# Moving the on-chip tiles of a two-block layer so that activation slots and weight buffers start at one place modulo 512 bytes

## The chip, the core and the metric

The kernel runs on one core of a Trainium2 chip. The metric is the device time of one execution in microseconds. A core has TensorE for matrix products (the profile splits it into PE, the matmuls, and PEld, the weight loads that run ahead of them), VectorE (DVE), ScalarE (ACT), GpSimd (POOL) and SyncE (SP), which only issues transfers here. Operands lie in the on-chip memory SBUF, whose 128 partitions all use the same byte address for one element of a tile; products are summed in PSUM.

## The reference

Two transformer-like blocks follow each other on 256 tokens of width 2048, all in float32. Nearly all the work is products of a 256-row activation with large weights:

```python
def first_block(x, p, w_in, ...):
    h = rmsnorm(x, g_mix[i])
    proj = h @ w_in[i]                       # 2048 x 10240
    y_sb = stick_breaking_attention(q_sb, k_sb, v_sb)
    y_ca = chunked_relpos_attention(q_ca, k_ca, v_ca, rel_bias[i])
    merged = (sigmoid(gate_sb) * (y_sb @ w_sb_out[i]) + sigmoid(gate_ca) * (y_ca @ w_ca_out[i]))
    x = x + merged @ w_mix_out[i]
    g_ff, u_ff = split(rmsnorm(x, g_ffn[i]) @ w_ffn_in[i], 2)      # 2048 x 11264
    x = x + (silu(g_ff) * u_ff) @ w_ffn_out[i]
    x = x + sigmoid(rmsnorm(x, g_ple[i]) @ w_ple_gate[i]) * (p[i] @ w_ple_in[i])
    return rmsnorm(x, g_final)

def second_block(x, ...):
    proj = rmsnorm_2(h, norm_mix_w[l]) @ w_in[l]                   # 2048 x 13328
    y_a, y_b, y_c = s5_branch(...), gla_branch(...), diff_attn_branch(...)
    merged = g0 * y_a + g1 * y_b + g2 * y_c
    h = h + merged @ w_out[l]
    h = h + conv_gated_mlp(rmsnorm_2(h, norm_ffn_w[l]), ffn_w_up[l], ..., ffn_w_down[l])
    return rmsnorm_2(h, norm_final_w)
```

## The kernel before

**The stream of weights.** All weights pass through one loop, `stream` (L448 to L537), in tiles of 128 x 1024 floats. SyncE loads a tile into one of four `raw` buffers (L459); ScalarE rounds it to a high part `wh`, one of five buffers (L466); VectorE takes the difference `wl`, one of four buffers (L476). TensorE then multiplies with the high and the low part, so that a product keeps more digits than one pass gives. These passes read `float32r` operands, at one column per step of the clock.

**The activations.** An activation is split in the same way and kept in slots of 8192 bytes in each partition, fifteen of them (`NSLOT = 15`, L187). A slot of class `Acts` holds four k-tiles, each as 256 columns of high part and 256 of low part. The same fifteen slots hold every other intermediate too. `try_slot` (L208) hands out the first free one, so which slot a product reads is fixed when the program is built.

**Two kinds of products.** A matmul reads two operands from SBUF: the stationary one, 128 columns, which a weight load puts into the array ahead of the matmul, and the moving one, up to 512 columns.

- Kind AS, `mm_as` (L555 to L562): the slot is stationary, the weight buffer is moving, 512 columns each; three matmuls for each k-tile and half (L560, L561, L562).
- Kind WS (L522 to L532): the weight buffer is stationary, the slot is moving; for each k-tile and half one matmul of 256 columns with `wl` (L530) and one of 512 columns with `wh` (L526).

While matmul number i streams its moving operand, the weight load of number i+1 reads its stationary operand: one of the two reads is always from a slot, the other from a `wh` or `wl` buffer.

**Where tiles lie.** Tiles get addresses pool by pool, in the order in which the pools are opened (L192 to L194): `one`, `raw`, `wh`, `wl`, `ev`. Within a pool tiles follow each other in the order of their first use, each rounded up to 32 bytes. The fifteen slots are tiles of the pool `one` (L212), which also holds small tiles (`r`, `rh`, `ss`, `nv`, `lam`: 8 to 48 bytes), the residual `big` (16384 bytes), the parameters `par` (L580, 832 bytes), constants `cst` (1536 bytes) and `tri`/`rel`/`conv` (L589, 1376 bytes). The slots therefore start at different places modulo 512, wherever a small tile came between.

Of the kernel before, what the change touches and what calls it, by code (L numbers as in the profile page):

```python
# [9 lines left out]
F32 = mybir.dt.float32  # L10
# [149 lines left out]
class Flag:  # L160


    def __init__(self, tile=None):
        self.tile, self.ready = tile, False
# [21 lines left out]
class Build:  # L186
    NSLOT = 15  # L187

    def __init__(self, tc, d, out, es):
        self.tc, self.nc, self.d, self.out = tc, tc.nc, d, out  # L190
        pool = lambda name, bufs, **kw: es.enter_context(tc.tile_pool(name=name, bufs=bufs, **kw))
        self.one = pool("one", 1)  # L192
        self.rawp, self.whp, self.wlp = pool("raw", RAWB), pool("wh", CA + 1), pool("wl", SA + 1)
        self.ev = pool("ev", 2)  # L194
        self.accp = pool("acc", 2, space=PSUM)
        self.psp = pool("ps", 1, space=PSUM)
        self.drp = pool("dr", 1, space=bass.MemoryType.DRAM)
        self.psfree, self.cooling, self.ticks = [0, 1, 2, 3], [], 0
        self.slotfree = list(range(self.NSLOT))
        self.gens, self.lanes, self.nm = [], {}, 0  # L200
        self.tab, self.forced, self.nrb = None, 0, 0
# [6 lines left out]
    def try_slot(self, shape, dtype=F32):  # L208
        if not self.slotfree:
            return None  # L210
        i = self.slotfree.pop(0)
        return self.one.tile(shape, dtype, tag=f"s{i}", name=self.name("s")), i  # L212

    def slot(self, shape, dtype=F32):
        while True:
# [209 lines left out]
        rb.ready = True  # L425

    def new_norm(self, with_rb=True):
        r = Flag(self.one.tile([128, 2], F32, tag=self.name("r"), name=self.name("r")))
        r.half = self.one.tile([128, 2], F32, tag=self.name("rh"), name=self.name("rh"))
        rb = None  # L430
        if with_rb:
            self.nrb += 1
            rb = Flag(self.one.tile([128, 256], F32, tag=f"rb{self.nrb % 2}", name=self.name("rb")))
        ss = self.one.tile([128, 2, 4], F32, tag=self.name("ss"), name=self.name("ss"))
        return r, rb, ss
# [141 lines left out]

    def consts(self):
        nc, d, one = self.nc, self.d, self.one
        self.par = one.tile([128, P_N], F32, tag="par", name="par")  # L580
        self.cst = one.tile([128, C_N], F32, tag="cst", name="cst")
        nc.sync.dma_start(out=self.par, in_=d["par"])
        c = self.cst
        self.ident, self.ones, self.BT = (c[:, o:o + 128] for o in (C_ID, C_ONE, C_BT))
        self.one1 = c[:, C_ONE:C_ONE + 1]
# [1182 lines left out]
```

## Time and profile before

| | |
|---|---|
| median of 3 runs | 3183.13 us (3182.76 to 3183.58) |
| the profiled execution, its own time | 3182.36 us |
| its span, first to last instruction | 3180.2 us |
| PE busy | 3161.4 us, 99% of the span |
| PEld busy | 2668.2 us, 84% |
| DVE busy | 1994.4 us, 63% |
| ACT busy | 1553.3 us, 49% |
| DMA engines, queue that SyncE issues on | 55.8% |
| matmuls of kind AS (L560, L561, L562) | 3 x 2372 |
| matmuls of kind WS (L526, L530) | 2 x 3936 |

Busy time is time in which at least one instruction of the engine is under way. The recorded duration of one matmul holds its way through the array as well, so that records overlap: what a matmul costs in a stream is the distance from its start to the next one's start, and a group's first and last start, divided by the number of steps between them, gives that distance.

### The profile page before, as it was taken

The numbers are of one execution on the slowest core, as the hardware profiler recorded it, in microseconds if no ns is written. First come the engines' busy times: TensorE is split into PE (matmuls) and PEld (weight loads), VectorE is DVE, ScalarE is ACT, GpSimd is POOL, SyncE is SP. The second block draws the span as 40 slices with busy tenths as digits, with TensorE's granted clock in tenths as the row PEclk, the third lists the DMA queues.
The fourth block names the chain that finished last, engine by engine and source line by source line (L and its number), as shares of the span: only waits on it lengthen the run. The fifth ranks groups of instructions, "written<-read, shape, count | busy, mean of one in ns | idle before, by whom it ended". The sixth has DMA issues, their size and how long they took to land.

```text
span 3180.2 us, 43735 instructions
## 1 busy us (share of the span) xinstructions
PE 3161.4 (99%) x16909; PEld 2668.2 (84%) x16909; DVE 1994.4 (63%) x2593; ACT 1553.3 (49%) x2035; POOL 72.5 (2%) x158
## 2 busy tenths in 40 slices
PE   8999999999999999999999999999999999999998
PEld 7888888888888888888888888878888888888887
DVE  5656445557577676566655657945555766757666
ACT  6544444455444454456544454434445644545545
POOL 0000000000001000000000001000000000000000
PEclk9999999999999999999999999999999999999999
DMA  7555555565667767555654565655555555555554
GB/s 263 168 176 166 185 188 183 180 187 186 216 223 246 243 225 238 186 175 190 210 178 159 170 214 192 211 183 198 197 183 182 186 192 185 186 195 185 189 185 165
DMA packets 172639, 617.90 MB, mean 194 GB/s; under 512 B 23552, under 2 KB 23968, under 8 KB 169232
## 3 DMA queue, kind: packets, MB, share of 16 engines
q1 hardware_dynamic: 164992, 577.49, 55.8%
q0 software_dynamic: 7440, 37.64, 3.5%
q8 instruction: 132, 2.16, 0.3%
q14 instruction: 75, 0.61, 0.1%
HBM read 599.74 MB, written 14.25 MB: 193 GB/s over the span
## 4 chain that ended last, share of the span: by engine, by line
PE 99%; ACT 0%; DMA 0%; DVE 0%; DVEq 0%; issue 0%; SPq 0%; ACTq 0%
PE acc L526 29%; PE acc L560 17%; PE acc L562 17%; PE acc L561 17%; PE acc L530 15%; PE p L346 1%; PE p L1673 0%; PE p L1132 0%; PE p L1713 0%; PE p L906 0%; PE p L908 0%; PE p L907 0%; PE p L1716 0%; PE p L1109 0%; PE p L1128 0%; PE p L1707 0%
## 5 line engine op out<-in xcount | busy, mean ns | idle before, releaser
L476 DVE TENSOR_TENSOR wl<-raw,wh 128x1024 fp32r<-128x1024 f32 x1088 | 1320.6, 1220 | 667.1 <-PE acc L561 446.0
L466 ACT CAST wh<-raw 128x1024 fp32r<-128x1024 f32 x1088 | 1138.9, 1049 | 1110.3 <-PE acc L562 672.1
L526 PE MATMUL acc<-s,wh 128*128 128x512 f32 x3936 | 1383.8, 396 | 0.0
L530 PE MATMUL acc<-s,wl 128*128 128x256 f32 x3936 | 1090.6, 282 | 0.0
L560 PE MATMUL acc<-wh,s 128*128 128x512 f32 x2372 | 939.0, 396 | 0.8 <-DVE big L1351 0.8
L562 PE MATMUL acc<-wh,s 128*128 128x512 f32 x2372 | 930.8, 392 | 0.0
L561 PE MATMUL acc<-wl,s 128*128 128x512 f32 x2372 | 930.3, 392 | 0.0
L526 PEld LDWEIGHTS acc<-s,wh 128*128 128x128 f32 x3936 | 734.1, 188 | 164.0
L530 PEld LDWEIGHTS acc<-s,wl 128*128 128x128 f32 x3936 | 741.7, 188 | 11.0 <-issue 1.0
L562 PEld LDWEIGHTS acc<-wh,s 128*128 128x128 f32 x2372 | 445.6, 188 | 99.9
L560 PEld LDWEIGHTS acc<-wh,s 128*128 128x128 f32 x2372 | 445.9, 188 | 99.2 <-issue 1.7
L561 PEld LDWEIGHTS acc<-wl,s 128*128 128x128 f32 x2372 | 446.0, 188 | 97.5 <-issue 0.5
L442 DVE TENSOR_TENSOR s<-acc,s 128x512 f32<-128x512 f32 (+1 forms) x120 | 82.7, 689 | 271.1 <-ACT s L441 271.0
L441 ACT COPY s<-acc 128x512 f32<-128x512 f32 (+1 forms) x120 | 70.0, 584 | 195.0 <-PE acc L526 192.8
L310 ACT ACTIVATE s<-s 128x256 f32<-128x256 f32 (+4 forms) x175 | 76.6, 443 | 105.2 <-DVE s L313 38.1
L313 DVE SCALAR_TENSOR_TENSOR s<-s,conv 128x256 f32<-128x256 f32 x172 | 79.4, 482 | 3.1
L444 DVE TENSOR_TENSOR s<-s,rb 128x512 f32<-128x512 f32 (+1 forms) x104 | 71.7, 690 | 3.5
L318 ACT CAST s<-s 128x256 fp32r<-128x256 f32 (+1 forms) x104 | 45.5, 442 | 30.4 <-DVE s L946 15.3
L1630 DVE TENSOR_TENSOR s<-s,s 128x1024 f32<-128x1024 f32 x48 | 58.5, 1219 | 0.0
L310 ACT ACTIVATE s<-s,conv 128x256 f32<-128x256 f32 x86 | 47.1, 595 | 22.5 <-DVE s L444 22.5
L319 DVE TENSOR_TENSOR s<-s,s 128x256 fp32r<-128x256 f32 (+1 forms) x104 | 47.4, 458 | 14.2 <-ACT s L318 13.0
L310 ACT ACTIVATE junk<-big 128x512 f32<-128x512 f32 x48 | 30.3, 632 | 50.0 <-DVE big L925 35.5
(265 smaller groups left out, 1034.5 us busy)
## 6 DMA issues: line engine op xcount, KB each, us to landing
raw<-in_w_fin SPq DMA_DIRECT2D x176, 512.0 KB, 4.3
raw<-in_w_up SPq DMA_DIRECT2D x172, 512.0 KB, 3.9
raw<-in_w_fout SPq DMA_DIRECT2D x88, 512.0 KB, 4.2
raw<-in_w_down SPq DMA_DIRECT2D x84, 512.0 KB, 4.0
raw<-in_w_qksb SPq DMA_DIRECT2D x32, 512.0 KB, 3.6
raw<-in_w_qkca SPq DMA_DIRECT2D x32, 512.0 KB, 3.4
raw<-in_w_gsb SPq DMA_DIRECT2D x32, 512.0 KB, 4.2
raw<-in_w_gca SPq DMA_DIRECT2D x32, 512.0 KB, 4.2
```

What stands on the lines that cost most here:

```text
L310: self.nc.scalar.activation(out, in_, func, scale=scale, **kw)
L313: self.nc.vector.scalar_tensor_tensor(out=out, in0=in0, scalar=scalar, in1=in1, op0=op0, op1=op1)
L441: nc.scalar.copy(out, acc[:, 0:n, 256:512])
L442: nc.vector.tensor_add(out, acc[:, 0:n, 0:256], out)
L444: nc.vector.tensor_mul(out, out, rb.tile[:, None, :].to_broadcast([128, n, 256]) if n > 1 else rb.tile[:, None, :])
L466: nc.scalar.copy(wh[:, :n] if j.kind != "W4" else wh[:, :n].bitcast(F32), raws[i][:, :n])
L476: nc.vector.tensor_sub(wl[:, :n], r[:, :n], wh[:, :n].bitcast(F32))
L526: hi = lambda: nc.tensor.matmul(acc[:, f, :], lhsT=wh[:, s], rhs=x, start=k == first, stop=k == end)
L530: nc.tensor.matmul(acc[:, f, 256:512], lhsT=wl[:, s], rhs=x[:, 0:256], start=False, stop=False)
L560: nc.tensor.matmul(acc[:, m, :], lhsT=xl, rhs=wh[:, s], start=k == first, stop=False)
L561: nc.tensor.matmul(acc[:, m, :], lhsT=xh, rhs=wl[:, s], start=False, stop=False)
L562: nc.tensor.matmul(acc[:, m, :], lhsT=xh, rhs=wh[:, s], start=False, stop=k == end)
```

## The change

No instruction is added, removed, moved or made to wait for something else; the built programs name the same instructions with the same waits in the same order on all engines. Three edits move tiles:

- the fifteen slots become tiles of a pool of their own, `slots`, opened after `one`;
- the two small tiles of a norm, `r` and its half, become one tile of 16 bytes, which saves 32 bytes for each norm;
- `par` is made 64 floats (256 bytes) longer; only its first 208 columns are used, as before.

```diff
-        self.one = pool("one", 1)
+        self.one, self.slotp = pool("one", 1), pool("slots", 1)
...
-        return self.one.tile(shape, dtype, tag=f"s{i}", name=self.name("s")), i
+        return self.slotp.tile(shape, dtype, tag=f"s{i}", name=self.name("s")), i
...
     def new_norm(self, with_rb=True):
-        r = Flag(self.one.tile([128, 2], F32, tag=self.name("r"), name=self.name("r")))
-        r.half = self.one.tile([128, 2], F32, tag=self.name("rh"), name=self.name("rh"))
+        t = self.one.tile([128, 4], F32, tag=self.name("r"), name=self.name("r"))
+        r = Flag(t[:, 0:2])
+        r.half = t[:, 2:4]
...
-        self.par = one.tile([128, P_N], F32, tag="par", name="par")
+
+        self.par = one.tile([128, P_N + 64], F32, tag="par", name="par")[:, 0:P_N]
```

The addresses that the built programs give, in bytes within a partition, and what is left modulo 512:

| tiles | before: addresses | modulo 512 | after: addresses | modulo 512 |
|---|---|---|---|---|
| 2 slots | 20256, 28448 | 288 | 40704, 48896 | 256 |
| 2 slots | 55392, 63584 | 96 | 57088, 65280 | 256 |
| 3 slots | 73152, 81344, 89536 | 448 | 73472, 81664, 89856 | 256 |
| 8 slots | 97760 to 155104 | 480 | 98048 to 155392 | 256 |
| `raw`, 4 buffers | 163552 to 175840 | 224 | 163584 to 175872 | 256 |
| `wh`, 5 buffers | 179936 to 196320 | 224 | 179968 to 196352 | 256 |
| `wl`, 4 buffers | 200416 to 212704 | 224 | 200448 to 212736 | 256 |
| `big` | 36640 | 288 | 20032 | 64 |

Within slots and buffers the operands of the stream begin at multiples of 512 bytes, so the table holds for every operand of L526, L530 and L560 to L562. Of the 2372 groups of three matmuls of kind AS, 1240 have their stationary operand in a slot at 480, 528 at 448, 444 at 96 and 160 at 288. Of the 3936 pairs of kind WS, 1880 read a slot at 480, 1040 at 288, 600 at 448 and 416 at 96.

## Rows read from the trace of the kernel before

**Rows 1.** The page's head: span; busy time, share and instructions by engine; the granted clock in 40 slices; the chain that ended last, by engine and by line.

```profile
span 3180.2 us, 43735 instructions
PE 3161.4 (99%) x16909; PEld 2668.2 (84%) x16909; DVE 1994.4 (63%) x2593; ACT 1553.3 (49%) x2035; POOL 72.5 (2%) x158
...
PEclk9999999999999999999999999999999999999999
...
PE 99%; ACT 0%; DMA 0%; DVE 0%; DVEq 0%; issue 0%; SPq 0%; ACTq 0%
PE acc L526 29%; PE acc L560 17%; PE acc L562 17%; PE acc L561 17%; PE acc L530 15%; PE p L346 1%; PE p L1673 0%; PE p L1132 0%; PE p L1713 0%; PE p L906 0%; PE p L908 0%; PE p L907 0%; PE p L1716 0%; PE p L1109 0%; PE p L1128 0%; PE p L1707 0%
```

**Rows 2.** What PE waited for in the whole span: engine, line, what ended the wait; us in total, times, longest.

```profile
PE acc L552 <- ACT wh L466: 8.6, 1, 8.6
PE acc L560 <- DVE big L1351: 0.8, 1, 0.8
```

**Rows 3.** The matmuls of L561 (kind AS, 512 columns) in four stretches, one answer each: count; duration in ns, shortest, median, longest; first and last start in us. In the first stretch the stationary operands lie in slots at 96 modulo 512, in the second at 448, in the third at 288, in the fourth at 480. L560 and L562 alternate with L561 in all four.

```profile
L561 PE MATMUL acc<-wl,s x16: 390/394/405, 183.7 to 194.2; 128*128 128x512 f32 x16
...
L561 PE MATMUL acc<-wl,s x16: 393/395/397, 194.9 to 205.4; 128*128 128x512 f32 x16
...
L561 PE MATMUL acc<-wl,s x16: 389/394/399, 2046.1 to 2056.6; 128*128 128x512 f32 x16
...
L561 PE MATMUL acc<-wl,s x94: 388/389/398, 1008.6 to 1071.9; 128*128 128x512 f32 x94
```

**Rows 4.** The four stretches of rows 3 and two of rows 5: busy us of each engine and its instructions, the granted clock as a share of 2.4 GHz, the mean share of the DMA engines, GB/s.

```profile
core 0: us, PE busy (x) PEld busy (x) DVE busy (x) ACT busy (x) POOL busy (x), PEclk, DMA share, GB/s
184.00:194.60 10.60, 10.60 (x47) 8.62 (x46) 4.90 (x4) 5.35 (x6) 0.00 (x0) 1.00 0.61 199
195.20:205.80 10.60, 10.60 (x47) 8.55 (x46) 4.90 (x4) 4.20 (x4) 0.00 (x0) 1.00 0.62 198
2046.40:2057.00 10.60, 10.60 (x47) 8.59 (x46) 10.08 (x24) 5.36 (x6) 0.00 (x0) 1.00 0.63 200
1008.00:1072.00 64.00, 64.00 (x284) 52.99 (x284) 43.06 (x39) 26.37 (x27) 5.79 (x10) 1.00 0.75 244
725.40:733.40 8.00, 8.00 (x47) 6.99 (x46) 4.90 (x6) 4.36 (x6) 0.00 (x0) 1.00 0.43 146
971.50:979.40 7.90, 7.90 (x47) 6.96 (x46) 4.80 (x6) 3.11 (x4) 1.80 (x4) 1.00 1.01 299
```

**Rows 5.** The matmuls of L526 (kind WS, 512 columns) in four stretches, in the same columns as rows 3; a matmul of L530 (256 columns) lies between each two. The moving operands lie in slots at 448 modulo 512 in the first stretch, at 288 in the second, at 480 in the third and fourth.

```profile
L526 PE MATMUL acc<-s,wh x15: 387/397/402, 59.9 to 64.8; 128*128 128x512 f32 x15
...
L526 PE MATMUL acc<-s,wh x16: 392/397/403, 2525.9 to 2531.2; 128*128 128x512 f32 x16
...
L526 PE MATMUL acc<-s,wh x24: 387/397/404, 725.1 to 733.2; 128*128 128x512 f32 x24
...
L526 PE MATMUL acc<-s,wh x24: 390/392/397, 971.3 to 979.3; 128*128 128x512 f32 x24
```

**Rows 6.** L561, L526 and L530 over the whole span, one answer each, in the columns of rows 3 (the last number of a row, its count of one form, is cut off by the view).

```profile
L561 PE MATMUL acc<-wl,s x2372: 386/390/405, 13.1 to 3170.2; 128*128 128x512 f32 x198
...
L526 PE MATMUL acc<-s,wh x3936: 386/396/588, 55.3 to 3131.2; 128*128 128x512 f32 x197
...
L530 PE MATMUL acc<-s,wl x3936: 273/281/471, 55.5 to 3131.1; 128*128 128x256 f32 x197
```

**Rows 7.** Matmuls of 256 columns of plain float32 (each product shows as two records), in the columns of rows 3: attention scores, L688 and L738, with both operands in one slot, and the spreading of a norm, L421, with the stationary operand at 96 and the moving one at 224 modulo 512.

```profile
L688 PE MATMUL p<-s x16: 377/377/379, 69.3 to 162.7; 128*128 128x256 f32 x16
...
L738 PE MATMUL p<-s x16: 379/381/382, 221.5 to 311.2; 128*128 128x256 f32 x16
...
L421 PE MATMUL p<-diag,cst x8: 377/378/380, 49.2 to 2458.9; 128*128 128x256 f32 x8
```

**Rows 8.** The page's groups for the steps that make `wl` and `wh`: count; busy us, mean ns of one; idle us of the engine just before them.

```profile
L476 DVE TENSOR_TENSOR wl<-raw,wh 128x1024 fp32r<-128x1024 f32 x1088 | 1320.6, 1220 | 667.1 <-PE acc L561 446.0
L466 ACT CAST wh<-raw 128x1024 fp32r<-128x1024 f32 x1088 | 1138.9, 1049 | 1110.3 <-PE acc L562 672.1
```

## The prediction

> **What bounds the kernel now.** I read the page's head first [rows 1]: TensorE is busy 99% of the span, its clock is granted in full (2.4 GHz) in all 40 slices, and the chain that ended last runs over PE alone, 95 of 100 parts of it over five lines: L526 and L530 (kind WS), L560, L561 and L562 (kind AS). Then what PE waited for [rows 2]: 8.6 us once at the start, 0.8 us once later. No transfer, cast or subtraction is late. So only one thing can move the time by much: the distance from one matmul's start to the next one's. Whether that distance depends on where the operands lie is the question, and the view for it is a line's matmuls in a stretch, with first and last start.
>
> In four stretches of kind AS, all steady, the slot differs and nothing else in the matmul does [rows 3]. A step is a third of the distance between two matmuls of L561. Slots at 96: 183.7 to 194.2 us over 15 x 3 steps, 10.5 / 45 = 233 ns. Slots at 448: 194.9 to 205.4, 233 ns. Slots at 288: 2046.1 to 2056.6, 233 ns. Slots at 480: 1008.6 to 1071.9 over 93 x 3 steps, 63.3 / 279 = 227 ns. The starts are printed to 0.1 us, so the first three are good to about 2 ns; the medians of the durations (394, 395, 394 against 389) say the same with 5 ns. I take 6 ns.
>
> It is not the other engines. VectorE is busy 46% of the first two stretches and 95% of the third, with the same 233 ns; it is busy 67% of the fourth, where the DMA engines are busiest (0.75) and the step is shortest [rows 4]. So it is the slot. Measured from the weight buffer at 224, the stationary operand begins 384, 224 and 64 bytes further on modulo 512 in the slow stretches and 256 in the fast one.
>
> **Weighed against the skill.** The Trainium skill, "TensorE: Matmul & The Clock Gate", section "Step-by-step: what each phase is for", says that PE has two independent read ports, and that loading the next weights takes no read bandwidth from the running matmul. By that rule the slots would make no difference and the sum would be zero. Rows 3 do not agree: 227 and 233 ns for the same instruction. This chip's trace decides, and the rule stays as a rival below.
>
> **The change part by part.** No instruction is added or taken away, and none waits for something else, so there is no cost of that kind, the merged norm tiles included. The longer `par` and the pool of its own only move addresses. DVE and ACT read and write moved tiles as well; if their steps became longer, L476 has 667 us and L466 has 1110 us of idle time just before its instructions, most of it waiting for PE to give a buffer back [rows 8], so a few per cent on 1320.6 and 1138.9 us stay hidden. The cover goes only where they get within a buffer's reach of PE, which rows 2 show nowhere after the start. `raw` moves by 32 bytes and its loads are not on the chain either. What is left is the reading of operands by PE. After the change the two operands are 0 apart modulo 512 in every matmul of the five lines, and no matmul of the trace shows that at this rate of columns. So it has to be bounded.
>
> - Kind AS, likeliest value: 0 apart behaves as 256 apart. Among the four distances it is the only one with 227 ns, and 224, which is just 32 bytes less, already has 233 ns: what makes the step short is met exactly, not nearly. A pattern that repeats every 256 bytes puts 0 in the same class as 256. 3 x 1240 = 3720 of the 7116 AS matmuls already run at 227 ns; the other 3396 gain 6 ns: 20.4 us.
> - Kind WS: the distance of a pair L526 and L530 is read from L526's starts [rows 5]. Slots at 448: 4.9 / 14 = 350 ns. Slots at 288: 5.3 / 15 = 353 ns. Slots at 480: 8.1 / 23 = 352 ns in one stretch and 8.0 / 23 = 348 ns in another, at the limit of the printing, but the medians 397 and 392 agree. So the same slots have two levels, and neither the slot nor the load explains it: the second stretch has the higher DMA share, 1.01 against 0.43 [rows 4]. Slots at 480 are again 256 from the buffers, with 348 to 352 ns where all others lie too. I take no change, with 3936 x 2.2 = 9 us either way.
> - The sum, against the profiled execution's own 3182.4 us, which lies 0.8 us under the median of the runs: 3182.4 - 20.4 = 3162.0, so 3163 us by the median.
>
> The bound from below: every matmul takes its line's shortest record. L526 386 instead of a median of 396, L530 273 instead of 281 [rows 6]: 3936 x 18 = 71 us; AS 386 instead of 389: 7116 x 3 = 21 us. Together 92 us under the forecast, 3071 us. The bound from above: AS at its longest record in a steady stretch, 405 instead of 390 (7116 x 15 = 107 us), L526 at 404 instead of 396 [rows 5, 6] (3936 x 8 = 31 us): 3183 + 138 = 3321 us. The likeliest value lies near neither end, since steady stretches sit within 6 ns of each other.
>
> For a floor the skill's same page, section "Wait — 56ns, not 53.3ns?", has 215.7 ns from start to start at 512 columns, and no stretch here comes to that. By it AS alone would give another 80 us, an estimate from that page.
>
> **The rivals.**
>
> 1. *Zero apart is one more of the ordinary distances.* Three of four distances tried have 233 ns; if 0 is like them, 3720 matmuls lose 6 ns: 22 us, 3205 us. For it: three to one, and that L738, whose operands are 0 apart, has 381 ns where L421, 384 apart, has 378 [rows 7]. Against it: L688 is 0 apart too and has 377. These are plain float32, 256 columns of which take nearly as long as 512 of the others, so they have room that the stream does not have. It decides from the mean: (3720 x 227 + 3396 x 233) / 7116 = 229.9 ns. An AS step above 230 ns makes the kernel slower. Worse than ordinary, with a step as long as the longest records, is the tail towards 3321.
> 2. *Zero apart is better than anything tried.* Both reads go to matching places always, and pairs of WS fall as well. For it: L530 and L526 have records of 273 and 386 in plenty of stretches, so shorter steps exist. Half of the 92 us: 3117 us.
> 3. *The place modulo 512 is not what counts.* The eight slots at 480 are also the eight highest addresses, from 97760 up; if the higher part of the memory is what makes them fast, the change keeps that as it was: 3183 us. For it: trace and addresses cannot separate the two. Against it: three slow classes far apart in address have one value, and the fast class begins at 97760, right above one that is slow. The skill's rule of independent ports would give the same 3183 us, and rows 3 speak against it.
>
> **How the numbers follow.** Forecast 0.40 (its own range 3150 to 3176, from the 9 us of WS and 2 ns on 3396 steps); slower rival 0.30, a quarter of it beyond 3212; better rival 0.20, a third of it below 3095; no difference 0.10. A measurement can tell about 0.2%, 6.4 us, from no change. Faster: 0.40 + 0.20, less 0.02 for forecasts that end within 6.4 us: 0.58. Same: 0.10 + 0.02 less 0.01: 0.11. Slower: 0.31. The range from 3095 to 3212 holds all but some 0.15.
>
> **What would show it.** Right: the median of L561 is 389 to 390 ns with a step of 227 ns in every stretch of kind AS, whatever slot it reads, and the four classes are gone; WS pairs stay at 348 to 353 ns; DVE's and ACT's waits for PE shrink together by no more than the span. Wrong: the AS step is 230 ns or above (rival 1), WS pairs fall below 345 ns (rival 2), or the same slots as before are slow and fast (rival 3). A wait of PE for L466 or L476 after the start would mean that the moved tiles cost the other engines something, which nothing in the profile announces.

## The result and the profile after

The changed kernel takes 3163.94 us (median of 4 runs, 3162.67 to 3164.47), the kernel before 3182.95 us beside it. The ratio is 0.994, with a 95% interval from 0.9923 to 0.9957: 19 us faster. The forecast was 3163 us.

The page's head of the changed kernel answers to [rows 1], and what PE waited for to [rows 2]. The added lines move the line numbers of the stream by one: L526 is L527 now, L530 is L531, L560 to L562 are L561 to L563, L476 is L477 and L466 is L467.

```profile
span 3161.8 us, 43735 instructions
PE 3143.7 (99%) x16909; PEld 2669.4 (84%) x16909; DVE 1993.5 (63%) x2593; ACT 1553.7 (49%) x2035; POOL 72.5 (2%) x158
...
PEclk9999999999999999999999999999999999999999
...
PE acc L527 29%; PE acc L561 17%; PE acc L562 17%; PE acc L563 17%; PE acc L531 15%; PE p L346 1%; PE p L1675 0%; PE p L1134 0%; PE p L1715 0%; PE p L908 0%; PE p L910 0%; PE p L909 0%; PE p L1718 0%; PE p L1111 0%; PE p L1130 0%; PE p L1709 0%
```

```profile
PE acc L553 <- ACT wh L467: 7.8, 1, 7.8
PE acc L561 <- DVE big L1353: 0.8, 1, 0.8
```

The number of instructions, the busy time of the other engines and the clock are as before. PE's busy time is shorter by 17.7 us of the 18.4 us that the span lost; of its waits the first is 0.8 us shorter and the other unchanged. The stretches of [rows 3], in the same order, with the `wl` matmul of kind AS:

```profile
L562 PE MATMUL acc<-wl,s x16: 388/390/390, 183.8 to 194.0; 128*128 128x512 f32 x16
...
L562 PE MATMUL acc<-wl,s x16: 388/390/390, 194.7 to 204.9; 128*128 128x512 f32 x16
...
L562 PE MATMUL acc<-wl,s x15: 388/390/390, 2036.3 to 2045.8; 128*128 128x512 f32 x15
...
L562 PE MATMUL acc<-wl,s x86: 388/390/390, 1007.7 to 1065.5; 128*128 128x512 f32 x86
```

The first three had medians of 394 to 395 ns and steps of 233 ns; now they have 390 ns and 10.2 / 45 = 227, 227 and 9.5 / 42 = 226 ns. The fourth had 227 ns and keeps them, 57.8 / 255. The scatter is gone as well: 388 to 390 where the first stretch had 390 to 405. Over the whole span, for [rows 6]:

```profile
L562 PE MATMUL acc<-wl,s x2372: 387/390/569, 13.5 to 3151.7; 128*128 128x512 f32 x198
...
L527 PE MATMUL acc<-s,wh x3936: 386/397/587, 54.8 to 3112.8; 128*128 128x512 f32 x197
...
L531 PE MATMUL acc<-s,wl x3936: 273/281/470, 55.0 to 3112.7; 128*128 128x256 f32 x197
```

The medians of kind WS have hardly moved: 397 and 281 ns, where 396 and 281 stood.

Where the time went is read from all starts of the two traces. A step is the time from a matmul's start to the start of the next one, and it is put down to the first of the two; steps with a small matmul of the attention or the scan in between, or with a wait, are left out. The mean AS step fell from 229.96 to 226.99 ns, which over 7116 steps is 21.1 us. In kind WS two shifts nearly cancel, which the medians do not show: the 512-column step rose from 233.1 to 234.6 ns and the 256-column step fell from 118.0 to 116.9 ns. The sum of the WS steps rose by 1.6 us. That makes 19.5 us, where the span lost 18.4 us; the 1.1 us between them are not put down to any line.

### The profile page after: what moved, and what is told of

It is laid out like the page before. It is cut to its first block, busy times and chain, and to the rows that moved or that the text cites. A ratio compares the mean times of both kernels' runs of the same rounds, so it can differ in the third digit from the quotient of the medians.

```text
span 3161.8 us, 43735 instructions
## 1 busy us (share of the span) xinstructions
PE 3143.7 (99%) x16909; PEld 2669.4 (84%) x16909; DVE 1993.5 (63%) x2593; ACT 1553.7 (49%) x2035; POOL 72.5 (2%) x158
## 4 chain that ended last, share of the span: by engine, by line
PE 99%; ACT 0%; DMA 0%; DVE 0%; DVEq 0%; issue 0%; SPq 0%; ACTq 0%
PE acc L527 29%; PE acc L561 17%; PE acc L562 17%; PE acc L563 17%; PE acc L531 15%; PE p L346 1%; PE p L1675 0%; PE p L1134 0%; PE p L1715 0%; PE p L908 0%; PE p L910 0%; PE p L909 0%; PE p L1718 0%; PE p L1111 0%; PE p L1130 0%; PE p L1709 0%
## 5 line engine op out<-in xcount | busy, mean ns | idle before, releaser
L477 DVE TENSOR_TENSOR wl<-raw,wh 128x1024 fp32r<-128x1024 f32 x1088 | 1320.4, 1220 | 651.1 <-PE acc L562 425.2
L467 ACT CAST wh<-raw 128x1024 fp32r<-128x1024 f32 x1088 | 1139.6, 1050 | 1091.2 <-PE acc L563 674.9
L527 PE MATMUL acc<-s,wh 128*128 128x512 f32 x3936 | 1385.2, 398 | 0.0
L531 PE MATMUL acc<-s,wl 128*128 128x256 f32 x3936 | 1091.1, 282 | 0.0
L561 PE MATMUL acc<-wh,s 128*128 128x512 f32 x2372 | 933.4, 394 | 0.8 <-DVE big L1353 0.8
L563 PE MATMUL acc<-wh,s 128*128 128x512 f32 x2372 | 924.9, 390 | 0.0
L562 PE MATMUL acc<-wl,s 128*128 128x512 f32 x2372 | 924.7, 390 | 0.0
L527 PEld LDWEIGHTS acc<-s,wh 128*128 128x128 f32 x3936 | 735.5, 188 | 165.2
L531 PEld LDWEIGHTS acc<-s,wl 128*128 128x128 f32 x3936 | 744.6, 189 | 11.1 <-issue 1.0
L563 PEld LDWEIGHTS acc<-wh,s 128*128 128x128 f32 x2372 | 445.8, 188 | 93.3
L561 PEld LDWEIGHTS acc<-wh,s 128*128 128x128 f32 x2372 | 446.0, 188 | 92.6 <-issue 1.6
L562 PEld LDWEIGHTS acc<-wl,s 128*128 128x128 f32 x2372 | 446.1, 188 | 90.6 <-issue 0.5
```

What stands on the lines that cost most here:

```text
L467: nc.scalar.copy(wh[:, :n] if j.kind != "W4" else wh[:, :n].bitcast(F32), raws[i][:, :n])
L477: nc.vector.tensor_sub(wl[:, :n], r[:, :n], wh[:, :n].bitcast(F32))
L527: hi = lambda: nc.tensor.matmul(acc[:, f, :], lhsT=wh[:, s], rhs=x, start=k == first, stop=k == end)
L531: nc.tensor.matmul(acc[:, f, 256:512], lhsT=wl[:, s], rhs=x[:, 0:256], start=False, stop=False)
L561: nc.tensor.matmul(acc[:, m, :], lhsT=xl, rhs=wh[:, s], start=k == first, stop=False)
L562: nc.tensor.matmul(acc[:, m, :], lhsT=xh, rhs=wl[:, s], start=False, stop=False)
```

## Experiments

Distances below are from the weight buffer to the slot for AS and from the slot to the weight buffer for WS, always from the moving to the stationary operand, modulo 512. Steps that are not read from a row are means over all starts of a line in that kernel's trace, sorted by the operands' addresses in the built program. The lettered theories are those of the expectations.

### Slots in their own pool, and nothing else

```diff
-        self.one = pool("one", 1)
+        self.one, self.slotp = pool("one", 1), pool("slots", 1)
...
-        return self.one.tile(shape, dtype, tag=f"s{i}", ...), i
+        return self.slotp.tile(shape, dtype, tag=f"s{i}", ...), i
```

> The kernel before with only the pool for the slots: slots and weight buffers both begin at 224 modulo 512, 0 apart, as far apart as in the changed kernel but not at a multiple of 256 (nor of 64). Theory A (only the distance between slot and weight buffer counts, and the pattern repeats every 256 bytes): the AS step is 227 ns in all slots, time 3164 us within 5. Theory B (the place itself counts: a read that begins at a multiple of 256 is fast): the AS step is 233 ns in all slots, 3720 x 6 = 22 us over the kernel before, 3205 us.

3163.61 us, ratio 0.9938 (0.9922 to 0.9955): the whole gain. One stretch of its `wl` matmul:

```profile
L561 PE MATMUL acc<-wl,s x81: 389/389/389, 1010.1 to 1064.5; 128*128 128x512 f32 x81
```

54.4 / 240 = 227 ns, with all operands at 224 modulo 512. Theory B falls: the place itself does not count. The longer `par` and the merged norm tiles, two of the change's three edits, add nothing that can be seen in the time.

### 128 bytes apart

```diff
+        pool("gap", 1).tile([128, 32], F32, tag="gap", name="gap")
         self.rawp, self.whp, self.wlp = pool("raw", RAWB), pool("wh", CA + 1), pool("wl", SA + 1)
```

> The changed kernel with 128 bytes left free between the slots and the raw buffers: slots stay at 256 modulo 512, weight buffers go to 384; 128 apart. Theory A: every AS step is 233 ns as in the slots at 96 of the kernel before, 7116 x 6 = 43 us over the changed kernel, 3206 us; the WS pairs are as in the slots at 96 of before or 2 ns shorter, so 3199 to 3208 us. Theory B (the place of the slot alone counts): 227 ns, 3164 us. Theory C (the layout's other effects made the gain): 3164 us.

3199.71 us, ratio 1.0053 (1.0038 to 1.0068): 36 us over the changed kernel, by 128 unused bytes. A short and the long stretch of AS, the second of which had been the fast one in all kernels so far:

```profile
L563 PE MATMUL acc<-wl,s x16: 390/392/404, 183.9 to 194.3; 128*128 128x512 f32 x16
...
L563 PE MATMUL acc<-wl,s x84: 390/393/404, 1011.6 to 1069.5; 128*128 128x512 f32 x84
```

57.9 / 249 = 233 ns in the slots with the highest addresses too. The mean AS step is 232.5 ns: 5.5 x 7116 = 39 us. The WS pair fell from 351.5 to 350.9 ns (230.8 + 120.1), 2 us. Theory A holds, theories B and C, which both had 3164 us, fall, and so does rival 3 of the prediction (the higher part of the memory).

### 256 bytes apart

The same edit with 64 floats for the gap and the longer `par` undone.

> The changed kernel without the longer par and with 256 bytes left free between slots and raw buffers: slots at 0, weight buffers at 256 modulo 512; 256 apart everywhere. Theory A: the AS step is 227 ns and WS pairs as in the changed kernel, 3164 us within 5. Theory D (0 apart and 256 apart are two different cases that happen to have one AS step): AS 227 ns, WS pairs may differ by 1 to 3 ns, 3160 to 3176 us.

3163.09 us, ratio 0.9937 (0.9922 to 0.9952).

```profile
L563 PE MATMUL acc<-wl,s x82: 389/389/389, 1009.9 to 1064.9; 128*128 128x512 f32 x82
```

55.0 / 243 = 226 ns, and the WS lines have 234.5 and 117.0 ns, as at 0 apart (234.6 and 116.9). For both kinds 0 and 256 are one case.

### A ladder of distances

```diff
         i = self.slotfree.pop(0)
+        if 0 < i < 14 and i not in self.stepped:
+            self.stepped.add(i)
+            self.slotp.tile([128, 8], F32, tag=f"step{i}", ...)      # 32 bytes
```

> The changed kernel without the longer par and with 32 bytes put between each slot and the next: the slots are 96, 128, 160, 192, 224, 256, 288, 320, 352, 384, 416, 448, 480, 0 and 0 bytes from the weight buffers modulo 512. Read by slot. Theory A: the AS step is 227 ns at 256 and 0 and 231 to 235 ns at all others, the same at two distances that differ by 256 (96 and 352, 128 and 384, 160 and 416, 192 and 448, 224 and 480); time some 3164 + 12/15 x 43 = 3198 us. Theory E (the fast case is a band around 0 and 256, not a point): neighbours at 32 bytes on one side are fast too. Theory D (period 512): distances that differ by 256 have different steps.

3187.14 us, ratio 1.0014 (1.0003 to 1.0024); 3198 were expected. Five stretches of its `wl` matmul, at 192, 224, 256, 384 and 0 apart (the first matmul of each still reads the slot before):

```profile
L565 PE MATMUL acc<-wl,s x8: 392/392/394, 448.5 to 453.4; 128*128 128x512 f32 x8
...
L565 PE MATMUL acc<-wl,s x8: 392/395/397, 454.0 to 458.9; 128*128 128x512 f32 x8
...
L565 PE MATMUL acc<-wl,s x7: 389/389/393, 459.6 to 463.7; 128*128 128x512 f32 x7
...
L565 PE MATMUL acc<-wl,s x8: 389/392/404, 465.1 to 470.0; 128*128 128x512 f32 x8
...
L565 PE MATMUL acc<-wl,s x15: 388/389/395, 590.8 to 600.4; 128*128 128x512 f32 x15
```

Eight matmuls are too few for a step from printed starts, since 0.1 us in 21 steps is 5 ns. The table has the mean steps over the whole trace in ns (AS: L564 to L566; WS: L530, 512 columns, and L534, 256 columns); the smallest cells hold about 100 starts:

| apart | 0 | 32 | 64 | 96 | 128 | 160 | 192 | 224 |
|---|---|---|---|---|---|---|---|---|
| AS | 227.5 | | | 233.9 | 232.9 | 233.3 | 229.9 | 233.2 |
| WS, 512 | | 230.6 | | 229.2 | 230.9 | 235.4 | 231.8 | |
| WS, 256 | | 118.3 | | 118.1 | 118.5 | 119.6 | 118.9 | |

| apart | 256 | 288 | 320 | 352 | 384 | 416 | 448 | 480 |
|---|---|---|---|---|---|---|---|---|
| AS | 227.3 | 233.1 | 233.2 | 233.9 | 232.7 | 233.4 | 229.4 | 233.3 |
| WS, 512 | 236.0 | 231.2 | 233.7 | 230.5 | 230.2 | 233.5 | | |
| WS, 256 | 117.1 | 118.1 | 118.2 | 117.6 | 119.5 | 117.7 | | |

For AS the lower table repeats the upper one within 0.7 ns wherever both have a value: the period is 256 bytes (theory D falls). 0 is fast, 32 bytes to either side of 256 is slow (224 and 288; theory E falls), and there is one more level that nobody had expected, 229 to 230 ns at 192 and 448. With the shorter WS steps that explains most of the 11 us under the expectation. In WS the order is another one: 512 columns are shortest at 96, longest at 256 and 160, and two distances that differ by 256 can lie 1.9 ns apart (160 and 416). The WS figures are rough, since one job reads four slots of different distances in turn.

### Only the low weights 128 apart, only the high weights 128 apart

The first kernel has a gap of 128 bytes between the pools `wh` and `wl`. The second has one before `wh` as well, which brings `wl` to 256 apart (its longer `par` is undone).

> The changed kernel with 128 bytes left free between the wh and the wl buffers, so that wl alone is 128 apart from the slots, wh stays 0 apart. Theory F (what counts in a step is the pair that is read at one time: the moving operand of matmul i and the stationary one of i+1): AS: L561, which streams wl, 233 ns, L560 and L562 227 ns. WS: the step of L526, during which wl is loaded for L530, is 231 ns as at 128 apart, the step of L530, during which wh is loaded, 117 ns as at 0 apart; the pair 348 instead of 351.5. Sum: + 2372 x 6 = 14 us and - 3936 x 3.6 = 14 us, so 3164 us within 6. Theory G (a step is set by its own matmul's two operands, not by the next one's load): AS the same, WS the other way round: L526 (own operand wh) 234.5, L530 (own operand wl) 120: + 14 + 12 = 3190 us.

> The counterpart: wh alone is 128 apart from the slots, wl 256 apart. Theory F: AS: L560 and L562 233 ns, L561 227 ns: + 4744 x 6 = 28 us. WS: L526 234.5 ns as at 0 or 256 apart, L530 120 ns as at 128 apart: + 3936 x 3 = 12 us; 3204 us within 6. Theory G: AS the same, L526 231 and L530 117: + 28 - 14 = 3178 us.

3193.93 us (1.0035, 1.0022 to 1.0048) and 3179.12 us (0.9988, 0.9978 to 0.9997). The totals are those of theory G, within 4 us and 1 us, but the steps are not:

| step in ns | AS, low with `wh` | AS, high with `wl` | AS, high with `wh` | WS, 512 | WS, 256 |
|---|---|---|---|---|---|
| changed kernel | 227.0 | 226.9 | 227.1 | 234.6 | 116.9 |
| `wl` 128 apart | 234.5 | 232.9 | 230.7 | 232.3 | 116.9 |
| `wh` 128 apart | 232.3 | 226.2 | 228.5 | 232.7 | 119.3 |

One stretch of the first kernel, the three matmuls of AS in their order:

```profile
L563 PE MATMUL acc<-wh,s x80: 397/398/398, 1014.6 to 1069.9; 128*128 128x512 f32 x80
...
L564 PE MATMUL acc<-wl,s x79: 394/395/396, 1014.9 to 1069.5; 128*128 128x512 f32 x79
...
L565 PE MATMUL acc<-wh,s x79: 392/393/393, 1015.1 to 1069.7; 128*128 128x512 f32 x79
```

The `wh` matmuls L563 and L565 read the same places, 0 apart, as in the changed kernel, and have 398 and 393 ns instead of 390. So a bad distance in one matmul lengthens the steps around it; neither theory had that for AS. In WS theory F has the direction right in the first kernel: `wl` is moved, and the 512-column step falls from 234.6 to 232.3 ns (231 were expected), although its own operands are `wh` and the slot; the 256-column step, whose own operand is `wl`, stays at 116.9 ns. In the second kernel theory F has the 256-column step nearly right (119.3, expected 120) and the other wrong (232.7, expected 234.5): there the step's own `wh` was moved.

That the totals met theory G was chance both times. In the first kernel AS lost 40.6 us (5.71 x 7116) where 14 were expected, and WS gained 9.5 us (2.4 x 3936) where theory G had a loss of 12. In the second AS lost 14 us where 28 were expected, and WS lost 2 us where theory G had a gain of 14. Nor do the costs add up: three AS steps in a row grow by 17 ns with `wl` alone 128 apart, by 6 ns with `wh` alone, and by 16 ns with both. So a sum of one price for each matmul's distance does not describe AS once the distances are mixed.

### The `wl` matmul last

The kernel with `wl` 128 apart, with the second and third matmul of AS exchanged:

```diff
-                nc.tensor.matmul(acc[:, m, :], lhsT=xh, rhs=wl[:, s], start=False, stop=False)
-                nc.tensor.matmul(acc[:, m, :], lhsT=xh, rhs=wh[:, s], start=False, stop=k == end)
+                nc.tensor.matmul(acc[:, m, :], lhsT=xh, rhs=wh[:, s], start=False, stop=False)
+                nc.tensor.matmul(acc[:, m, :], lhsT=xh, rhs=wl[:, s], start=False, stop=k == end)
```

> The kernel with wl alone 128 apart, in which the three matmuls of kind AS stand in another order: low part of the slot with wh, high part with wh, high part with wl. There the step from the wh matmul to the wl matmul was 234.5 ns, from wl to the next wh 233, from wh to wh 231. Theory J (the reads run ahead of the recorded starts, so the step before the wl matmul is lengthened too, whichever matmul it is): now the second step (high with wh) is 234 to 235 ns, the third (wl) 233, the first (low with wh) 231; time 3194 us within 5. Theory K (it belongs to the matmul with the low part of the slot): the first step stays at 234 to 235.

3193.22 us, ratio 1.0043 (1.0017 to 1.0068). The mean steps are 230.9 (low with `wh`), 233.7 (high with `wh`) and 232.5 ns (high with `wl`). So on average the longest step moved from the first matmul to the second, again the one ahead of the `wl` matmul, as theory J says and theory K does not. But the mean mixes two patterns that each last for whole stretches. In 71 of 100 groups of three the second step is the longest, most often with 236 ns; in 26 the first one is, as theory K has it. The stretch shown above for the order before is one of those:

```profile
L563 PE MATMUL acc<-wh,s x80: 392/394/398, 1014.8 to 1069.6; 128*128 128x512 f32 x80
...
L564 PE MATMUL acc<-wh,s x80: 391/394/396, 1015.0 to 1069.8; 128*128 128x512 f32 x80
...
L565 PE MATMUL acc<-wl,s x79: 390/394/395, 1015.3 to 1069.4; 128*128 128x512 f32 x79
```

The medians of the durations are equal there; from the starts the three steps are 233.0, 230.7 and 229.6 ns. In the order before, too, the first step is the longest in only 74 of 100 groups, and the third in 25. Distances and order are the same in both patterns, so they do not decide alone. Theory J fits the larger part and is not shown; what chooses the pattern is open.

### WS with its low weights 96 bytes further on

By the ladder and the changed kernel 96 apart is the best distance of the 512-column step of WS, and 0 or 256 apart the best of everything else. By theory F only `wl` has to move for it, and only for jobs of kind WS. Two kinds in one set of buffers need buffers of two widths, with the start chosen by kind, so that `wl` lies 96 or 352 bytes from the slot in WS and 0 or 256 in AS (to make room, `par` has its old length again and more small norm tiles are merged; the pool of `wl` is opened with `pool("wl", 1)`, since its four buffers have names of their own now):

```diff
-                wl = self.wlp.tile([128, 1024], F32R, tag="wl", ...)
+                odd, ws = i % 2, j.kind == "WS"
+                o = (0 if ws else 40) if odd else (24 if ws else 0)
+                wl = self.wlp.tile([128, 1064 if odd else 1048], F32R, tag=f"wl{i % 4}", ...)[:, o:o + 1024]
```

> The changed kernel, in which only matmuls of kind WS take wl from 96 bytes further on, in enlarged wl buffers (two small norm tiles more are merged and the longer par is undone for room); AS reads all operands 0 or 256 apart. In the ladder L526 was shortest at 96 apart (229.2 ns against 234.5) and L530 at 0 apart (117.0). Theory F: L526 falls to 229 to 230 ns, L530 stays at 117, AS at 227: - 3936 x 5 = 20 us, 3144 us. Theory G: L530 goes to 118 and L526 stays at 234.5: 3168 us. Theory H (a WS pair as a whole lies at one of two levels that the ladder mixed): gain below 8 us, 3156 to 3164 us.

3150.53 us (3149.78 to 3151.13), ratio 0.9898 (0.9882 to 0.9915): 32 us under the kernel before and some 13 us under the changed kernel, between theory F (20 us) and theory H (under 8 us). A WS stretch of the changed kernel, then the same stretch of this one:

```profile
L527 PE MATMUL acc<-s,wh x30: 387/398/404, 969.8 to 980.0; 128*128 128x512 f32 x30
...
L531 PE MATMUL acc<-s,wl x29: 277/282/286, 970.0 to 979.9; 128*128 128x256 f32 x29
```

```profile
L529 PE MATMUL acc<-s,wh x30: 392/392/397, 969.9 to 979.9; 128*128 128x512 f32 x30
...
L533 PE MATMUL acc<-s,wl x30: 278/278/288, 969.8 to 979.8; 128*128 128x256 f32 x30
```

Medians of 398 and 282 ns became 392 and 278. Over the whole trace the 512-column step is 231.1 ns instead of 234.6 (not the 229.2 of the ladder), the 256-column step 117.0 instead of 116.9, AS 227.0 as before: 3.5 x 3936 = 14 us. The step that got shorter is that of the matmul whose own operands stay 0 apart; what was moved against the slot is the weight that is loaded while it runs. The mean is again a mixture: pairs of a 512-column and a 256-column step of 359 ns and more are 23 of 100 in the changed kernel and none here, pairs of at most 348 ns 25 of 100 there and 83 here. Theory H is right that a pair has levels, and wrong that little is to be gained from them.

## Why the prediction was right

- **What bounds the kernel.** Right. All but 0.8 us of the change lies in the distance from start to start, and the time followed it to within 2 us.
- **A gain in AS of 6 ns on 3396 steps, 20.4 us.** Right in size and in place: 21.1 us, and the stretches at 96, 448 and 288 came down to that at 480. The rows behind it were not quite pure: two of the 16 matmuls of each of the first three stretches in [rows 3] read a slot of another class. Sorted by slot, all starts of the kernel before give 232.7, 233.2 and 233.2 ns for the slots at 96, 448 and 288 and 227.2 ns for those at 480, so the reading stands.
- **0 apart is like 256 apart.** This was the choice on which the sign hung, made from four distances of which only one was fast. The kernel with 256 apart and the ladder show it: 227.3 against 227.5 ns, and every other pair of distances that differ by 256 agrees within 0.7 ns. The argument that 32 bytes less than 256 were already slow held up as well (233.2 at 224, 233.1 at 288). But that argument gives a sharp point, not a period: a pattern of 512 bytes, with 0 as slow as the rest, would have fitted [rows 3] as well. The step from 256 to 0 was a guess that came out, and the forecast's chance of 0.40 had left room for that.
- **WS without change, within 9 us.** Right in the sum, 1.6 us more, and in part by luck: the 512-column step became 1.5 ns longer and the 256-column step 1.1 ns shorter, which the pair hides.
- **Nothing for the other engines.** Right: DVE 1993.5 and ACT 1553.7 us busy where 1994.4 and 1553.3 stood, and no new wait of PE. The steps that make `wl` and `wh` keep their length, and the idle time just before them shrinks by 16 and 19 us, about what the span lost. Their waits for PE that the rows name shrink by 18 us together (446.0 to 425.2 and 672.1 to 674.9 us; [rows 8] has them before):

```profile
L477 DVE TENSOR_TENSOR wl<-raw,wh 128x1024 fp32r<-128x1024 f32 x1088 | 1320.4, 1220 | 651.1 <-PE acc L562 425.2
L467 ACT CAST wh<-raw 128x1024 fp32r<-128x1024 f32 x1088 | 1139.6, 1050 | 1091.2 <-PE acc L563 674.9
```

- **Rival 1 (zero apart is ordinary)** would have been 3205 us. It is what 128 apart turned out to be, with 3200 us.
- **Rival 2 (better than anything tried)** did not come: the mean AS step is the 227 ns that 480 had, and the WS pair did not fall. A shorter kernel exists, but by another distance for one operand.
- **Rival 3 (not the place modulo 512)** fell twice: in the changed kernel the low slots are fast, and 128 apart the high ones are slow.
- **The Trainium skill's rule.** That the load of the next weights takes no read bandwidth from the running matmul (the Trainium skill, "TensorE: Matmul & The Clock Gate", "Step-by-step: what each phase is for") does not agree with these runs: in the last experiment the 512-column step fell by 3.5 ns, and of the distances between its operands only that of the weights loaded meanwhile had changed.

What stays open is the mechanism. The runs show which distances cost, and that the distance between operands counts and not their place. That the cost arises between two operands read at about the same time fits the last experiment, and is argued rather than shown. The runs do not show what it is that repeats every 256 bytes, why 192 is half as bad, how a bad distance of one matmul reaches its neighbours in AS, or what chooses between the patterns of steps in one and the same layout. Distances below 32 bytes were not tried.

## What to carry to other kernels

Where TensorE is busy all the time, look at the time between matmul starts by the tile that they read, not at the busy share: equal instructions with two steps point to a gain that the busy share (99% before and after) does not show. Here it was enough to keep a slot and a weight buffer a multiple of 256 bytes apart, which a pool of its own for the slots did by itself, because all slots and buffers are multiples of 512 bytes long. Which distance is best depends on the kind of product. When a layout is tested, move one group of tiles against the other, and read the steps one by one: a total can agree with a wrong theory.

## What the runs showed that was not expected

- 128 unused bytes between two pools cost 36 us of 3164, 1.1%.
- The two kinds of matmul want different distances: AS has its shortest step at 0 and 256 (227 ns), while the 512-column step of WS is among its longest there (234 to 236 ns against 229 to 231 with 96).
- AS has a third level, 229 to 230 ns, at 192 and 448.
- One layout can have two patterns of steps, each for whole stretches: with `wl` alone 128 apart and last in the order, 233, 231 and 230 ns in one stretch and most often 230, 236 and 234 ns elsewhere.
- VectorE, ScalarE and the transfers, which read and write the same memory, leave no mark on an AS step: over all starts of the changed kernel it is 227.0 ns with VectorE busy throughout and 227.1 with VectorE idle, 227.0 either way for ScalarE, and 227.0 with the DMA engines over 90% busy against 227.1 below 20%.
